# The delta rule's triangular inverses as 64x64 blocks on the array's quarters, in a two-block transformer kernel

## The chip, the core and the metric

The kernel runs as one program on one core of a Trainium2 chip. The core has five engines that run their own instruction streams in order and meet through semaphores: TensorE (PE; its weight loads are listed as PEld), VectorE (DVE), ScalarE (ACT), GpSimd (POOL) and SyncE (SP, which issues the DMAs here). The metric is the device time of one execution in microseconds (us), lower is better.

## The reference, cut to what matters

The program is two transformer blocks on 256 tokens of width 1024. The first (attention and a product-key expert layer) is not touched. In the second, half of the heads are a gated delta rule, computed in chunks of 64 tokens; the other half are a causal sliding window. This is the delta rule, and the window's scores:

```python
# q, k, v: (B, 8 heads, N = 4 chunks, 64 tokens, 64); beta, g: (B, 8, 4, 64)
G = jnp.cumsum(g, axis=-1)
decay = jnp.exp(jnp.where(causal, G[..., :, None] - G[..., None, :], -jnp.inf))
kb = k * beta[..., None]
A = jnp.where(strict, jnp.einsum('bhncd,bhnsd->bhncs', kb, k) * decay, 0.0)
L = A + jnp.eye(64)
rhs = jnp.concatenate([v * beta[..., None], kb * jnp.exp(G)[..., None]], axis=-1)
u, w = split(lax.linalg.triangular_solve(L, rhs, left_side=True, lower=True, unit_diagonal=True))
qk = jnp.where(causal, jnp.einsum('bhncd,bhnsd->bhncs', q, k) * decay, 0.0)
# then, chunk after chunk (state S of 64 x 64 per head):
v_new = u_c - w_c @ S;  o = q_dec_c @ S + qk_c @ v_new;  S = S * dec_c + k_dec_c.T @ v_new
...
# window: 8 query heads, 2 key heads, blocks of 128 queries over their own and the block of keys before
s = einsum(q, k) / 8 - slope_h * dist;  p = exp(s - m) / (sum + exp(sink - m));  o = p @ v
```

There are 8 heads x 4 chunks = 32 unit lower-triangular matrices of 64x64 to invert.

## The kernel before, in words

The tokens lie in two blocks `b` of 128, so a block holds two chunks of 64. Everything is float32; the large products are split in two parts `hi` and `lo` of a rounded type, at L95 and L96, and take three products each (L115 to L117 and L123 to L125). A float32 product of the small kind stands as one instruction in the program and as two matmul records in the trace, each with its weight load; a transpose stands as one and one.

The stretch at issue lies between the projections of the second block and its output projection:

- `conv` (L1006) and what follows it make k, v and q of the delta rule. ScalarE runs SiLU there, and the exponentials are held back behind `zsilu` by `issue_after`.
- L1091 to L1110 make the decay matrices: `Dm` (rows by columns of a block of 128, both chunks in one 128x128 matrix with zero corners) and its transpose `DT`, by products with `ones`, exponentials (L1104) and transposes (L1109).
- `inverse(b, hf, pool)` inverts the eight matrices of block `b` and of four heads (those with the parity `hf`) in 128x128 matrices, two chunks on the diagonal of each. It is a generator that other work is woven into. It starts with k times k transposed (L1147), A (L1153), A's transpose (L1157) and q times k (L1160). Then come five levels, n = 2, 4, 8, 16, 32: a product with A's transpose (L1181) and a mask on VectorE (L1183), a product with the transposed inverse so far (L1188) and a subtraction from T (L1189); T is turned on TensorE (L1174) and copied by ScalarE (L1175). It ends with u and w (L1197, L1198), copied at L1199 and L1200.
- Two such generators, hf = 0 and 1, run in turn (`together`), first for b = 0, then for b = 1.
- `aside` is the window attention in steps: `heads` (L1257) and `window` (L1289: scores L1301 and L1304, maximum L1307, exponentials L1316, division on GpSimd L1321, transposes L1327, product with v L1331). The first ASTEPS of its steps are woven into the inverses of b = 0, the rest into those of b = 1.
- `recur(b)` (L1210) runs the two chunks of a block: L1222 and L1231 with the state, L1237 and L1246 with v_new. `recur(0)` is woven into the inverses of b = 1, `recur(1)` into the window half of the output projection.

A scheduler orders each engine's instructions by what the program order and the pools allow; engines then follow that order. PSUM tiles come from rings: `ps_acc` 4, `ps_mm` 2, `ps_tr` 2. The reciprocal square roots are powers on GpSimd (L142).

Of the kernel before, what the change touches and what calls it, by code (L numbers as in the profile page):

```python
# [10 lines left out]
F32 = mybir.dt.float32  # L11
# [12 lines left out]
D = 1024  # L24
# [5 lines left out]
def tile_kernel(ctx: ExitStack, tc: tile.TileContext, a, out):  # L30
# [792 lines left out]
    for c in range(NCH):  # L823
# [23 lines left out]
        if c == 32:  # L847
# [27 lines left out]
            low = tri("low", BF, 0.0, NEG, True, False)  # L875
# [4 lines left out]
            def half(name, n, first=False):  # L880
                t = cst.tile([128, 64], F32, name=name)
                nc.gpsimd.memset(t, 1.0)
                v = t.rearrange("p (q i) -> p q i", i=n)
                lo, hi = (0, n - 1) if first else (n, 2 * n - 1)
                nc.gpsimd.affine_select(v, v, pattern=[[-2 * n, 64 // n], [0, n]], compare_op=OP.is_ge, fill=0.0,
                                        base=-lo, channel_multiplier=1)
                nc.gpsimd.affine_select(v, v, pattern=[[2 * n, 64 // n], [0, n]], compare_op=OP.is_ge, fill=0.0,
                                        base=hi, channel_multiplier=-1)
                return t

            pair_t = half("pair_t", 1, True)
            halves = {n: half("half%d" % n, n) for n in (1, 2, 4, 8, 16, 32)}
# [71 lines left out]
    with tc.tile_pool(name="b2", bufs=1) as b2:  # L964
# [126 lines left out]
        Dm = b2.tile([128, 2, 8, 128], F32, name="Dm")  # L1091
        DT = b2.tile([128, 2, 8, 128], F32, name="DT")
        for b in range(2):
            gt = b2.tile([128, 4, S], F32, tag="sc", name="gt", bufs=2).rearrange("p h k -> p (h k)").rearrange("p (h t) -> p h t", h=8)
            nc.gpsimd.tensor_tensor(gt, up[:, None, :].to_broadcast([128, 8, 128]),
                                    ngd[:, b, :, None].to_broadcast([128, 8, 128]), op=OP.mult)
            for hf in range(2):
                ps = ps_tr([128, 4, 128])
                nc.tensor.matmul(ps, ones, gt[:, hf * 4:hf * 4 + 4], start=True, stop=False)
                nc.tensor.matmul(ps, identb, low[:, None, :].to_broadcast([128, 4, 128]), start=False, stop=True)  # L1100
                for i in range(4):
                    h = hf * 4 + i
                    with tc.issue_after(zsilu.ins):
                        nc.scalar.activation(Dm[:, b, h], ps[:, i], AF.Exp, bias=Gc[:, b, h:h + 1])  # L1104
        for b in range(2):
            for hf in range(2):
                ps = ps_tr([128, 4, 128])
                for i in range(4):
# [428 lines left out]
```

## Time and profile before

| | |
|---|---|
| three runs | 1450.46, 1441.31, 1449.96 us; median 1449.96 |
| the profiled execution | 1448.03 us, span 1446.3 us |
| busy share of the span: PE, PEld, DVE, ACT, POOL | 94%, 81%, 76%, 51%, 25% |
| matmul records | 8918 |
| DMA, share of 16 engines' span | 52.8% |
| granted TensorE clock | 0.984 of full speed on average |

The busy share of PE is a union of records that overlap, each with its way through the array, so it says that TensorE always had something in flight, and not that it was at its peak. The shares are averages over stages; the stretch of the delta rule and the window lies at about 1100 to 1210 us of the span.

### The profile page before, as it was taken

The numbers are of one execution on the slowest core, as the hardware profiler recorded it, in microseconds if no ns is written. First come the engines' busy times: TensorE is split into PE (matmuls) and PEld (weight loads), VectorE is DVE, ScalarE is ACT, GpSimd is POOL, SyncE is SP. The second block draws the span as 40 slices with busy tenths as digits, with TensorE's granted clock in tenths as the row PEclk, the third lists the DMA queues.
The fourth block names the chain that finished last, engine by engine and source line by source line (L and its number), as shares of the span: only waits on it lengthen the run. The fifth ranks groups of instructions, "written<-read, shape, count | busy, mean of one in ns | idle before, by whom it ended". The sixth has DMA issues, their size and how long they took to land.

```text
span 1446.3 us, 24961 instructions
## 1 busy us (share of the span) xinstructions
PE 1355.2 (94%) x8918; PEld 1178.5 (81%) x8918; DVE 1104.1 (76%) x2345; ACT 741.7 (51%) x1577; POOL 361.1 (25%) x295
## 2 busy tenths in 40 slices
PE   6778799999899999999999999999989999899998
PEld 5535589999899999998777778777787887799997
DVE  7988786889889999978777777788687475755555
ACT  4436455555455544456555555455566233555553
POOL 2224333575633333334101010111143210000000
PEclk9999899999999999999999999999999999999999
DMA  9822255545454545458787788787243002355552
GB/s 360 298 93 99 99 164 169 180 160 175 154 167 162 161 150 172 147 175 304 245 269 262 253 277 274 261 303 258 79 129 119 16 1 88 123 189 184 190 184 79
DMA packets 79389, 259.33 MB, mean 179 GB/s; under 512 B 11680, under 2 KB 15776, under 8 KB 79264
## 3 DMA queue, kind: packets, MB, share of 16 engines
q1 hardware_dynamic: 79264, 257.74, 52.8%
q8 instruction: 70, 1.15, 0.3%
q14 instruction: 55, 0.45, 0.1%
HBM read 256.65 MB, written 1.05 MB: 178 GB/s over the span
## 4 chain that ended last, share of the span: by engine, by line
PE 61%; DVE 17%; DMA 10%; issue 6%; ACT 3%; POOL 3%; DVEq 0%; POOLq 0%; ACTq 0%; SPq 0%
PE ps_mm L123 11%; PE ps_mm L125 10%; PE ps_mm L124 10%; DMA raw<-in_w_ada_dram 6%; PE ps_acc L117 5%; PE ps_acc L115 5%; PE ps_acc L116 5%; DVE lo L96 4%; DVE raw L185 4%; PE ps_tr L730 2%; DMA raw<-in_expert_v_dram 2%; PE ps_acc L1188 1%; PE ps_acc L1181 1%; ACT hi L95 1%; DVE xl L846 1%
## 5 line engine op out<-in xcount | busy, mean ns | idle before, releaser
L95 ACT ACTIVATE hi<-raw 128x512 fp32r<-128x512 f32 (+3 forms) x772 | 473.3, 623 | 398.4 <-PE ps_mm L124 187.4
L96 DVE TENSOR_TENSOR lo<-raw,hi 128x512 fp32r<-128x512 f32 (+2 forms) x614 | 450.6, 745 | 151.5 <-ACT hi L95 147.1
L125 PE MATMUL ps_mm<-hh,lo 128*128 128x256 f32 x1600 | 450.6, 282 | 8.9 <-POOL lo L96 5.9
L123 PE MATMUL ps_mm<-hh,hi 128*128 128x256 f32 x1600 | 454.6, 284 | 2.2 <-DVE hh L235 1.9
L124 PE MATMUL ps_mm<-hl,hi 128*128 128x256 f32 x1600 | 450.5, 282 | 0.0
L96 POOL TENSOR_TENSOR lo<-raw,hi 128x512 fp32r<-128x512 f32 (+1 forms) x158 | 228.7, 1449 | 609.2 <-ACT hi L95 561.6
L125 PEld LDWEIGHTS ps_mm<-hh,lo 128*128 128x128 f32 x1600 | 302.7, 189 | 12.2 <-POOL lo L96 7.4
L123 PEld LDWEIGHTS ps_mm<-hh,hi 128*128 128x128 f32 x1600 | 303.1, 190 | 4.1 <-DVE hh L235 2.5
L124 PEld LDWEIGHTS ps_mm<-hl,hi 128*128 128x128 f32 x1600 | 302.9, 189 | 1.1
L117 PE MATMUL ps_acc<-hi,xl 128*128 128x512 f32 x512 | 203.0, 396 | 8.1 <-DVE xl L846 8.1
L116 PE MATMUL ps_acc<-lo,xh 128*128 128x512 f32 x512 | 202.1, 395 | 2.7 <-DVE lo L96 1.6
L115 PE MATMUL ps_acc<-hi,xh 128*128 128x512 f32 x512 | 201.5, 393 | 0.0
L185 DVE SCALAR_TENSOR_TENSOR raw<-raw,cact 128x1024 f32<-128x1024 f32 x86 | 114.2, 1331 | 49.9 <-DMA raw<-in_w_ada_dram 49.5
L117 PEld LDWEIGHTS ps_acc<-hi,xl 128*128 128x128 f32 x512 | 96.1, 188 | 35.5 <-DVE xl L846 14.5
L116 PEld LDWEIGHTS ps_acc<-lo,xh 128*128 128x128 f32 x512 | 96.2, 188 | 28.0 <-DVE lo L96 3.8
L115 PEld LDWEIGHTS ps_acc<-hi,xh 128*128 128x128 f32 x512 | 96.2, 188 | 21.4
L846 DVE TENSOR_TENSOR xl<-W,xh 128x256 fp32r<-128x256 f32 x128 | 65.1, 511 | 8.0 <-ACT xh L845 7.9
L845 ACT ACTIVATE xh<-W 128x256 fp32r<-128x256 f32 x128 | 52.0, 410 | 37.4 <-PE ps_acc L116 34.8
L117 PE MATMUL ps_acc<-hi,sl 128*128 128x512 f32 x120 | 47.7, 399 | 0.5 <-DVE sl L1371 0.5
L115 PE MATMUL ps_acc<-hi,sh 128*128 128x512 f32 x120 | 47.8, 400 | 0.0
L116 PE MATMUL ps_acc<-lo,sh 128*128 128x512 f32 x120 | 47.5, 396 | 0.0
L739 ACT ACTIVATE W<-ps_tr 128x64 f32<-128x64 f32 (+26 forms) x78 | 20.7, 291 | 47.2 <-DVE W L735 37.5
(402 smaller groups left out, 1787.2 us busy)
## 6 DMA issues: line engine op xcount, KB each, us to landing
raw<-in_expert_u_dram SPq DMA_DIRECT2D x128, 512.0 KB, 3.8
raw<-in_expert_v_dram SPq DMA_DIRECT2D x128, 512.0 KB, 4.5
raw<-in_w_ada_dram SPq DMA_DIRECT2D x96, 512.0 KB, 4.7
raw<-in_w_gate_dram SPq DMA_DIRECT2D x22, 512.0 KB, 3.3
raw<-in_w_up_dram SPq DMA_DIRECT2D x22, 512.0 KB, 3.2
raw<-in_w_down_dram SPq DMA_DIRECT2D x22, 512.0 KB, 3.2
raw<-in_w_out_dram SPq DMA_DIRECT2D x16, 512.0 KB, 3.5
raw<-in_w_query_dram SPq DMA_DIRECT2D x16, 512.0 KB, 3.7
```

The source lines that it names most:

```text
L95: nc.scalar.activation(hi[:, :n], raw[:, c0:c1], AF.Copy)
L96: sub = eng.tensor_sub(lo[:, :n], raw[:, c0:c1], hi[:, :n].bitcast(F32))
L115: nc.tensor.matmul(ps, xh, wh, start=start, stop=False)
L116: nc.tensor.matmul(ps, xh, wl, start=False, stop=False)
L117: nc.tensor.matmul(ps, xl, wh, start=False, stop=stop)
L123: nc.tensor.matmul(ps, wh, hh[:, k], start=k == 0, stop=False)
L124: nc.tensor.matmul(ps, wh, hl[:, k], start=False, stop=False)
L125: nc.tensor.matmul(ps, wl, hh[:, k], start=False, stop=k == KT - 1)
L185: nc.vector.scalar_tensor_tensor(w, w, 1.0, act, op0=OP.mult, op1=OP.mult, accum_out=acc)
L730: nc.tensor.matmul(ps[:, i], o2[:, q + i], o[:, q + i], start=n == 0, stop=n == 1)
L845: nc.scalar.activation(xh, W[:, c], AF.Copy)
L846: nc.vector.tensor_sub(xl, W[:, c], xh.bitcast(F32))
```

## The change

The inverses no longer stand in 128x128 matrices. A block's two chunks lie on the two halves of the partitions, all eight heads in columns of 64, and every product of the inverse is one 64x64 block of one head and one chunk, 16 of them (`tiles4`) to a product of all. The rows of the array that a product uses are set by the partition half of its inputs, the columns by the partition half of its output; the order of `tiles4` takes another quarter with every product. Outputs of the two row halves go to two PSUM tiles. `inverse(b, pool)` treats all eight heads, so there is one generator per block and no longer two. T is turned as a whole at each level; the last turn is a product with the identity, block by block. The decay matrix is made transposed and folded at once, with beta as a second one (`bDT`); A and its transposes are gone. The window's two key heads run in pairs, with scores and products alternating over halves of the array, and ASTEPS is 16 instead of 19.

```diff
+            def folded(name, t, n=64, dt=F32):
+                f = cst.tile([128, n], dt, name=name)
+                nc.gpsimd.tensor_tensor(f, t[:, :n], t[:, n:], op=OP.add)
+                return f
...
-                        nc.scalar.activation(Dm[:, b, h], ps[:, i], AF.Exp, bias=Gc[:, b, h:h + 1])
-        for b in range(2):
-            for hf in range(2):
-                ps = ps_tr([128, 4, 128])
-                for i in range(4):
-                    nc.tensor.transpose(ps[:, i], Dm[:, b, hf * 4 + i], ident)
-                nc.scalar.activation(DT[:, b, hf * 4:hf * 4 + 4], ps, AF.Copy)
+        nc.vector.tensor_scalar(nG, Gc, -1.0, None, op0=OP.mult)
+        sb = small.tile([128, 2, 8], F32, tag="sb", name="sb", bufs=1)
+        with tc.issue_after(zsilu.ins):
+            nc.scalar.activation(sb, gd, AF.Exp)
+        nc.vector.tensor_tensor(sb, sb, beta, op=OP.mult)
...
+            nc.gpsimd.tensor_tensor(gt, spread8(up64, 64), ngd[:, b, :, None].to_broadcast([128, 8, 64]), op=OP.mult)
+            nc.gpsimd.tensor_tensor(bt, spread8(id64, 64), beta[:, b, :, None].to_broadcast([128, 8, 64]), op=OP.mult)
+            ps = ps_tr([128, 8, 64])
+            nc.tensor.matmul(ps, chunk1, gt, start=True, stop=False)
+            nc.tensor.matmul(ps, identb, spread8(past, 64), start=False, stop=True)
+            for h in range(8):
+                with tc.issue_after(zsilu.ins):
+                    nc.scalar.activation(DT[:, b, h], ps[:, h], AF.Exp, bias=nG[:, b, h:h + 1], scale=-1.0)
+            ps = ps_tr([128, 8, 64])
+            nc.tensor.matmul(ps, chunk1, bt, start=True, stop=True)
+            nc.vector.tensor_tensor(bDT[:, b], ps, DT[:, b], op=OP.mult)
...
+        TWO = range(2)
+        P64 = [slice(i * 64, i * 64 + 64) for i in TWO]
+        tiles4 = [(p, i, c) for p in range(4) for i in TWO for c in TWO]
...
-        def inverse(b, hf, pool):
...
+        def inverse(b, pool):
+            ck = [slice(b * 128 + c * 64, b * 128 + c * 64 + 64) for c in TWO]
+
+            def of_keys(other):
+                ps = [ps_acc() for _ in TWO]
+                for p, c, i in tiles4:
+                    nc.tensor.matmul(ps[i][P64[c], p * 64:(p + 1) * 64], kF[P64[i], p, ck[c]], other[P64[i], p, ck[c]],
+                                     start=True, stop=True)
+                return [t[:, :256].rearrange("p (h t) -> p h t", h=4) for t in ps]
+
+            kk = of_keys(kF)
...
+            for i in TWO:
+                nc.vector.tensor_tensor(M[:, i::2], kk[i][:, :, ::2], first1[:, b, i::2], op=OP.mult)
+            nc.vector.tensor_tensor(T[:, :, ::2], T[:, :, ::2], M, op=OP.subtract)
+            for i in TWO:
+                nc.vector.tensor_tensor(AT[:, i::2], kk[i], bDT[:, b, i::2], op=OP.mult)
             yield
...
             for n in (2, 4, 8, 16, 32):
...
+                pt = ps_acc()
+                for p in range(4):
+                    nc.tensor.transpose(pt[:, p * 128:(p + 1) * 128], T[:, 2 * p:2 * p + 2].rearrange("p h t -> p (h t)"), ident)
+                TT = mat("TT", pool).rearrange("p h t -> p (h t)")
+                nc.scalar.activation(TT, pt, AF.Copy)
+                ps = [ps_acc() for _ in TWO]
+                M = b2.tile([128, 4, 2, 32], F32, tag="part", name="part", bufs=2)
+                for p, i, c in tiles4:
+                    nc.tensor.matmul(ps[c][P64[i], p * 32:(p + 1) * 32], AT[P64[c], 2 * p + i], cols(T, n)[P64[c], 2 * p + i],
+                                     start=True, stop=True)
+                for c in TWO:
+                    nc.vector.tensor_tensor(M[:, :, c], ps[c][:, :128].rearrange("p (h t) -> p h t", h=4),
+                                            halves[n][:, None].to_broadcast([128, 4, 32]), op=OP.mult)
                 yield
...
+                for p, c, i in tiles4:
+                    nc.tensor.matmul(ps[i][P64[c], 128 + p * 32:160 + p * 32],
+                                     TT[P64[i], p * 128 + c * 64:p * 128 + c * 64 + 64], M[P64[i], p, c], start=True, stop=True)
+                for i in TWO:
+                    t = cols(T, n)[:, i::2]
+                    nc.vector.tensor_tensor(t, t, compact(ps[i][:, 128:256], n), op=OP.subtract)
                 yield
...
+            for h in range(8):
+                for c in TWO:
+                    nc.tensor.matmul(pt[c][P64[c], h * 64:h * 64 + 64], T[P64[c], h], id64[P64[c]], start=True, stop=True)
+            nc.scalar.activation(TT[P64[0]].rearrange("p h t -> p (h t)"), pt[0][P64[0]], AF.Copy)
+            nc.vector.tensor_copy(TT[P64[1]].rearrange("p h t -> p (h t)"), pt[1][P64[1]])
             yield
...
+            for p, i, c in tiles4:
+                nc.tensor.matmul(pw[c][P64[i], p * 64:(p + 1) * 64], kbe[P64[c], b, 2 * p + i], TT[P64[c], 2 * p + i],
+                                 start=True, stop=True)
+            for c in TWO:
+                nc.scalar.activation(wT[:, :, ck[c]], pw[c][:, :256].rearrange("p (h t) -> p h t", h=4), AF.Copy)
+            pu = [ps_acc() for _ in TWO]
+            for h in range(8):
+                for c in TWO:
+                    nc.tensor.matmul(pu[c][P64[c], h * 64:h * 64 + 64], TT[P64[c], h], vb[P64[c], b, h], start=True, stop=True)
+            for c in TWO:
+                nc.vector.tensor_copy(u[P64[c], b], pu[c][P64[c]])
             yield
...
+                for jj in range(2):
+                    ps = [ps_mm([128, 2, S]) for _ in TWO]
+                    for i in range(2):
+                        for g in TWO:
+                            nc.tensor.matmul(ps[g][:, i, :nk], qT[P64[g], 2 * jj + i, t], kT[P64[g], :nk],
+                                             start=True, stop=True)
...
-        first = inverse(0, 0, b2), inverse(0, 1, b2)
+        first = inverse(0, b2)
...
-        together(inverse(1, 0, dr), inverse(1, 1, dr), r0, aside)
+        together(inverse(1, dr), r0, aside)
...
-ASTEPS = 19
+ASTEPS = 16
```

What the scheduler makes of it, at three places. First TensorE in two levels of the inverses of b = 1. Before (L1181 and L1188 are the products, four of one hf and four of the other, L1174 the turns, L1301 the window's scores, L1327 its transposes):

```order
L1181 MATMUL ps_acc<-T,AT 128x64 x4
L1174 MATMUL ps_acc<-ident,T 128x128 x4
L1181 MATMUL ps_acc<-T,AT 128x64 x4
L1174 MATMUL ps_acc<-ident,T 128x128 x4
L1188 MATMUL ps_acc<-part,TT 128x64 x8
L1181 MATMUL ps_acc<-T,AT 128x64 x4
L1174 MATMUL ps_acc<-ident,T 128x128 x4
L1181 MATMUL ps_acc<-T,AT 128x64 x4
L1174 MATMUL ps_acc<-ident,T 128x128 x4
L1188 MATMUL ps_acc<-part,TT 128x64 x8
```

and now (L1186 turns, L1192 and L1199 products, L1356 the window's transposes, L1361 its product with v):

```order
L1186 MATMUL ps_acc<-ident,T 128x128 x4
L1192 MATMUL ps_acc<-T,AT 64x32 x16
L1356 MATMUL ps_tr<-ident,sc 128x128 x4
L1199 MATMUL ps_acc<-part,TT 64x32
L1356 MATMUL ps_tr<-ident,sc 128x128 x2
L1199 MATMUL ps_acc<-part,TT 64x32 x15
L1356 MATMUL ps_tr<-ident,sc 128x128 x2
L1361 MATMUL ps_mm<-PT,kv 64x512
L1186 MATMUL ps_acc<-ident,T 128x128 x4
L1192 MATMUL ps_acc<-T,AT 64x32 x16
```

Where two halves took turns, one group of 16 now follows the other, with the window's work between the two products of a level.

Second VectorE at the start of b = 1, from the window's scores to the recurrence's first v_new (L1304 scores, L1307 and L1309 to L1312 maximum, L1319 and L1320 the sums, L1153 A, L1163 and L1164 the first level, L1223 v_new). Before:

```order
L1153 SCALAR_TENSOR_TENSOR A<-ps_acc,beta,Dm 128x128 x4
L1304 SCALAR_TENSOR_TENSOR sc<-dist,ps_mm 128x256
L1319 TENSOR_TENSOR sums<-sums,es 128x4
L1304 SCALAR_TENSOR_TENSOR sc<-dist,ps_mm 128x256
L1320 RECIPROCAL sums<-sums 128x4
L1153 SCALAR_TENSOR_TENSOR A<-ps_acc,beta,Dm 128x128
L1307 TENSOR_REDUCE mneg<-sc 128x4
L1153 SCALAR_TENSOR_TENSOR A<-ps_acc,beta,Dm 128x128
L1309 TENSOR_TENSOR mneg<-mneg,sinkB 128x4
L1163 TENSOR_TENSOR part<-A,half_9214 128x256
L1311 TENSOR_TENSOR es<-sinkB,mneg 128x4
L1223 TENSOR_TENSOR vn<-u,ps_tr 64x512
```

and now (L1328 scores, L1333 maximum, L1172, L1173 and L1175 the start of the inverse, L1247 v_new, L1256 the next product with the state):

```order
L1328 SCALAR_TENSOR_TENSOR sc<-dist,ps_mm 128x256 x8
L1333 TENSOR_REDUCE mneg<-sc 128x4
L1172 TENSOR_TENSOR part<-ps_acc,first_12967 128x4x32 x2
L1175 TENSOR_TENSOR AT<-ps_acc,bDT 128x4x64
L1173 TENSOR_TENSOR T<-T,part 128x256
L1175 TENSOR_TENSOR AT<-ps_acc,bDT 128x4x64
L1247 TENSOR_TENSOR vn<-u,ps_tr 64x512
L1333 TENSOR_REDUCE mneg<-sc 128x4
L1256 TENSOR_TENSOR u<-ps_tr,eq 64x512
```

The rows now are without a break: all eight scores of the window's second block and one maximum stand ahead of the inverse's start. Before, the four scores of one key head were woven into the making of A, and the other four came later.

Third ScalarE in the convolutions: now an exponential for `sb` (L1104) stands among the SiLUs (L1022).

```order
L95 ACTIVATE hi<-raw 128x512
L1104 ACT_TABLE_LOAD
L1104 ACTIVATE sb<-gd 128x16
L1017 ACTIVATE cx<-ps_mm 128x256
L1019 ACTIVATE cy<-ps_mm,convw 128x256
L1022 ACT_TABLE_LOAD
L1022 ACTIVATE F<-cy 128x256
```

Before, the first exponential came behind the last SiLU; two table loads are new here.

## Rows read from the trace of the kernel before

**Rows 1.** Busy time by stretch: stretch, length, busy (instructions) per engine, PE clock, DMA

```profile
1103.00:1121.00 18.00, 17.98 (x92) 12.38 (x91) 13.68 (x31) 12.41 (x32) 10.20 (x10) 1.00 0.26 89
1121.00:1155.00 34.00, 33.49 (x263) 29.79 (x262) 16.38 (x50) 9.95 (x27) 8.01 (x8) 1.00 0.05 17
1155.00:1210.00 55.00, 53.49 (x414) 43.80 (x413) 33.52 (x90) 19.18 (x55) 8.14 (x6) 1.00 0.00 1
```

**Rows 2.** Chain of waits, one level for b = 1: start, length, engine, line

```profile
1185.66 0.89 PE ps_acc L1181 x8
...
1188.28 1.73 PE ps_acc L1188 x16
1190.02 0.89 PE ps_acc L1181 x8
```

**Rows 3.** Chain of waits, marks of the two inverses' stretches

```profile
1121.89 0.17 PE ps_acc L1181 x2
...
1154.91 0.36 PE ps_acc L1198 x2
...
1179.91 1.03 PE ps_acc L1181 x8
...
1203.71 0.26 PE ps_acc L1197 x2
...
1210.36 1.02 PE ps_tr L1222 x8
```

**Rows 4.** Chain of waits, hand-overs between TensorE and VectorE in a level

```profile
1145.01 0.43 DVE T L1189
...
1145.49 0.66 PE ps_acc L1174 x4
```

**Rows 5.** Chain of waits, recurrence of b = 0, second chunk

```profile
1175.69 1.08 PE ps_tr L1237 x8
1176.78 1.07 PE ps_tr L1246 x16
```

**Rows 6.** Timeline of PE: start, length, line, form (rows*columns of the array)

```profile
1165.46 0.27 PE L1237 MATMUL ps_tr<-vn,kd 64*128 64x128 f32 x1
1165.46 0.27 PE L1160 MATMUL ps_acc<-F,kF 64*128 64x128 f32 x1
...
1163.78 0.59 PE L1331 MATMUL ps_mm<-PT,kv 128*64 128x512 f32 x1
1163.79 0.38 PE L1231 MATMUL ps_tr<-Sb,F 128*64 128x128 f32 x2
```

**Rows 7.** Groups by form, 1040 to 1250: count, busy, mean ns, idle before

```profile
L1189 DVE TENSOR_TENSOR T<-T,ps_acc 128x256 f32<-128x256 f32 x20 | 8.4, 421 | 8.9 <-PE ps_acc L1188 8.8
L1304 DVE SCALAR_TENSOR_TENSOR sc<-dist,ps_mm 128x256 f32<-128x256 f32 x8 | 3.1, 418 | 0.5 <-PE ps_mm L1301 0.5
L1223 DVE TENSOR_TENSOR vn<-u,ps_tr 64x512 f32<-64x512 f32 x4 | 2.7, 684 | 2.3 <-PE ps_tr L1222 2.3
L1307 DVE TENSOR_REDUCE mneg<-sc 128x4 f32<-128x1024 f32 x2 | 2.4, 1211 | 0.0
L1304 DVE SCALAR_TENSOR_TENSOR sc<-dist,ps_mm 128x128 f32<-128x128 f32 x8 | 1.9, 283 | 3.8 <-PE ps_mm L1301 3.8
L142 POOL TENSOR_TENSOR rstd<-ms,mhalf 128x10 f32<-128x10 f32 x2 | 4.3, 2138 | 4.1 <-DVE ms L141 4.1
L1016 ACT ACT_TABLE_LOAD x1 | 1.3, 1283 | 0.0
```

**Rows 8.** Chain of waits, decay matrices and start of b = 0

```profile
1110.19 1.08 PE ps_acc L1147 x8
1111.27 1.02 PE ps_tr L1109 x8
...
1117.55 1.08 PE ps_acc L1160 x8
```

**Rows 9.** Timeline of ACT in the convolutions, with idle time before

```profile
1078.39 0.42 ACT L1016 ACTIVATE F<-cy 128x256 f32<-128x256 f32 x1 [0.92 <-DVE cy L1015]
```

More of the change, by code (lines that the diff above doesn't have):

```diff
@@ L1105, in tile_kernel @@
-        for b in range(2):
-            for hf in range(2):
-                ps = ps_tr([128, 4, 128])
-                for i in range(4):
-                    nc.tensor.transpose(ps[:, i], Dm[:, b, hf * 4 + i], ident)
-                nc.scalar.activation(DT[:, b, hf * 4:hf * 4 + 4], ps, AF.Copy)
+        DT = b2.tile([128, 2, 8, 64], F32, name="DT")
+        bDT = b2.tile([128, 2, 8, 64], F32, name="bDT")
+        first1 = b2.tile([128, 2, 8, 32], F32, name="first1")
+        nG = small.tile([128, 2, 8], F32, tag="nG", name="nG", bufs=1)
@@ L1292, in window @@
                 nk = 128 * (b + 1)
-                po = ps_mm()
-                for g in range(2):
-                    hp = slice(g * 64, g * 64 + 64)
-                    sc = b2.tile([128, 4, S], F32, tag="sc", name="sc", bufs=2)
-                    mneg = small.tile([128, 4], F32, tag="mneg", name="mneg", bufs=2)
-                    for jj in range(2):
-                        ps = ps_mm([128, 2, S])
-                        for i in range(2):
-                            nc.tensor.matmul(ps[:, i, :nk], qT[hp, 2 * jj + i, t], kT[hp, :nk], start=True, stop=True)
+                sc = [b2.tile([128, 4, S], F32, tag="sc", name="sc", bufs=2) for _ in TWO]
@@ L1314, in window @@
-                    sums = small.tile([128, 4], F32, tag="sums", name="sums", bufs=2)
+                            nc.vector.scalar_tensor_tensor(sc[g][:, 2 * jj + i, :nk], dist[:, 256 - nk:],
+                                                           -(2.0 ** -(h + 1)), ps[g][:, i, :nk], op0=OP.mult, op1=OP.add)
+                    yield
+                mneg, es, sums = (small.tile([128, 8], F32, tag=n, name=n, bufs=2) for n in ("mneg", "es", "sums"))
+                for g in TWO:
+                    nc.vector.tensor_reduce(mneg[:, g * 4:g * 4 + 4], sc[g][:, :, :nk], axis=AX.X, op=OP.max)
@@ L1330, in window @@
                         yield
[L1331 removed]
+                    for g in TWO:
+                        nc.tensor.matmul(po[P64[g]], kv[:, kb, 128 + g * 64:192 + g * 64], PT[g], start=kb == 0, stop=kb == b)
                 nc.scalar.activation(oT[:, :, t], po.rearrange("p (j t) -> p j t", j=4), AF.Copy)
@@ L1339, in tile_kernel @@
             if k in (3, 6):
-                for g in first:
-                    next(g)
+                next(first)
         share["pool"] = 0.0
@@ L1346, in tile_kernel @@
         dr = tc.alloc_tile_pool(name="dr", bufs=1, side="right")
-        together(*first, (next(aside, None) for _ in range(ASTEPS)))
+        together(first, (next(aside, None) for _ in range(ASTEPS)))
         r0 = recur(0)
-        together(inverse(1, 0, dr), inverse(1, 1, dr), r0, aside)
+        together(inverse(1, dr), r0, aside)
         dr.release()
@@ L1441 @@
 GT = 8
-PARTS = 4
 ASHARE = 0.34
```

150 lines of the change are left out of this document (52 added, 98 removed).

## The prediction, written before the changed kernel was run

> **What bounds the kernel now.** I read the page's slices first: TensorE is busy in nearly all of them, so only a stretch in which its own work shrinks, or in which it waits in small steps, can move the time. Then the table by stretch [rows 1]: in the decay matrices and the start of b = 0 TensorE is busy for 17.98 of 18.00 us, in the inverses of b = 0 for 33.49 of 34.00 and in those of b = 1 for 53.49 of 55.00, with VectorE at 33.52 there; the clock is at its upper level, 2.4 GHz, throughout (1.00). So the kernel is bound by TensorE's instructions here, and not by their waits: two halves take turns and cover each other's masks. Then the chain of waits, for one level [rows 2]: from 1185.66 to 1190.02 us, 4.36 us, in which only TensorE rows stand. Then its marks [rows 3]: the inverse's work for b = 0 runs from 1121.89 to the end of L1198 at 1155.27 (33.4 us); from there to the first L1181 of b = 1 at 1179.91 it is 24.6; from there to L1197 at 1203.71 it is 23.8; and 6.65 more to L1222 of the last recurrence at 1210.36. Last the timeline, for what two blocks of the array do at once [rows 6].
>
> The profiled execution took 1448.03 us, 1.9 below the median of the three runs (1449.96, between 1441.31 and 1450.46). The sum goes against 1448.03.
>
> **The price of a small product.** Sixteen records of L1246 (eight products of 64x64 over 64 columns, one block of the array) take 1.07 us, and eight records with a 128-wide block take 1.08 [rows 5]: 67 ns for a record of the first kind, 135 for the second. L1237 and L1160 use different row halves and start in one instant, 1165.46, with the same 0.27 us each; L1331 and L1231, on different column halves, start 0.01 us apart [rows 6]. So two blocks work at once. Four at once, in turn with every product, stand in no row. A group of 16 products is 32 records: 2.14 us if one follows the other, 1.07 with pairs at once, 0.54 with all four. 32 columns in place of 64 I cost like 64, since a record's weights stay as many. I take 1.07, for pairs are what the rows show, and keep 0.54 and 2.14 as bounds.
>
> **A level.** Transposes 0.66 [rows 4], product 1.07, two masks of half the size (0.28 each by the 128x128 form, L1304) [rows 7], product 1.07 and 0.2 until its last result is out (a record lasts 0.27 [rows 6] and the next starts 0.07 later), two subtractions 0.57, and four hand-overs of 0.03 to 0.05 (L1189 ends at 1145.44, TensorE starts at 1145.49 [rows 4]): 0.66 + 1.07 + 0.57 + 1.27 + 0.57 + 0.16 = **4.30 us**, against 4.36 now. One generator per block means that TensorE has nothing of the inverse to do under masks and subtractions, some 1.3 us a level; the window's and recurrence's work fills part. So the gain in products is given back level by level as waiting. The change must gain elsewhere.
>
> **Part by part.**
> (a) Decay matrices and start of b = 0, TensorE full. Gone: 16 transposes L1109 at 1.02 per eight [rows 8], 2.0 us; eight of L1157, 1.0. L1147 and L1160, 8 products each for all heads, are 32 records at 1.08 per eight [rows 8], 4.3 us, and become two groups, 2.1. That is 5.2; the modes that now alternate with 128-wide work cost a little. I take −5, bounds −3 and −6. VectorE (13.68 of 18) and ScalarE (12.41) cover their new and lost passes [rows 1].
> (b) Inverses of b = 0, 33.4 now. After: five levels 21.5. The end: turn by a group 1.27, copy 0.68 (64x512 form of L1223 [rows 7]) and two hand-overs 0.1, then pw and pu 2.14: 4.2. In VectorE's stream the two heads' reciprocal square roots, powers of 2.14 us on GpSimd (L142) [rows 7], stand ahead of the subtractions of the first two levels; half of each lies under the product, so 2.3 more with its hand-overs. The window's own steps (scores, exponentials ahead of the copy of TT, GpSimd's division ahead of the transposes, the product with v) lie partly in the path: no row gives it for the new order; between 0 and GpSimd's whole 8.01 us of this stretch [rows 1] I take 4.0, the middle. Sum 32.0, so −1.4 (bounds −5.4 and +2.6).
> (c) From there to the first level of b = 1, 24.6 now: two generators, the recurrence's first chunks and the window's scores run through VectorE one behind the other. After, in the order shown: eight scores 3.1 (0.42 each), two maxima 2.4, the start (two of 0.28, three of 0.42) 1.8, v_new, its next product and o 3 x 0.68 = 2.05, four passes of 0.42 for the state and q times k 1.7 [rows 7]: 11.1. Then a first mask and the products that it lets through: 0.57 + 0.05 + 1.27, and L1237 and L1246, 2.15 [rows 5]: 4.0. Sum 15.1, so **−9.5**. A's passes are gone. The cover for all this is that nothing new waits ahead of them; without it, see the second rival.
> (d) Levels of b = 1, 23.8 now. After: four more levels 17.2, the turn 2.05, one power on GpSimd 2.0, the window's transposes and product with v 2.5 (estimates, bounded as in (b)): 23.75, so 0.
> (e) End of b = 1, 6.65 now: pw 1.27, hand-over 0.03, two copies at 0.4 each: 2.1, so −4.5; u is needed later.
> (f) ScalarE loads its table of functions twice more, since `sb` stands among SiLUs: 1.28 us a load [rows 7], 2.6. ScalarE idles between 0.9 us waits on VectorE there [rows 9], so part is hidden: +2.0, bounds 0 and 2.6.
> SyncE's DMA order stays; GpSimd loses the copies and updates of TT, which are not in the path. What comes behind, output projection and feed-forward, stays. Sum: −5 − 1.4 − 9.5 − 0 − 4.5 + 2.0 = −18.4, so 1429.6: **1430**, by its own bounds 1422 to 1439. Chance 0.42.
>
> **Rivals.**
> First: all four quarters at once. A group takes 0.54; 27 groups lie in the path, 20 in the levels and seven others (two in (a), three in (b), one each in (d) and (e)), so 27 x 0.53 = 14.3 less, of which the powers' waits of (b) and (d), 2.3 and 2.0, take 4.3 back, since the products that cover them are shorter: −10 on the forecast, **1420**. For it: row pairs and column pairs both run freely [rows 6]. Against: no more than two records stand together in these rows. Chance 0.25. The Trainium skill, "TensorEngine Tiling (Array Packing)", Theoretical Speedup and Tiling Configurations, lists four independent 64x64 tiles; no row of before shows four.
> Second: the change does not bring what it says, because the in-order streams keep (c) as long as it is: VectorE's eight scores and a maximum (4.6 us) now stand ahead of the inverse [rows 7], and the window's and recurrence's chains wait for one another. Then (c) gives 0 and the rest −8.9: **1439**. For it: 33.5 of 55 us of VectorE are busy in this stretch [rows 1]. Against: A's passes, 16 of them, go. Chance 0.16.
> Third, the other side: quarters do not overlap. A group costs 2.14, so the 27 groups add 28.9, of which the 4.3 of the powers' waits are covered: +24.6, **1454**, slower than before. It decides from a group of about 1.9 us (119 ns a product): there (18.4 + 4.3) / 27 = 0.84 are added to 1.07. For it: alternating modes at L1198 take 0.36 us for two records [rows 3], more than 0.27. Against: the pairs [rows 6]. Chance 0.15. The Trainium skill, "TensorEngine Tiling (Array Packing)", Instruction Overhead, speaks against the change: it states some 60 cycles for each product however few its columns, and that no tiling factor should be taken from a dimension that is already small, which 64 columns cut to 32 are. By that rule a group saves nothing for its 32 columns, and the sum is 1430, as I have it; were the cost in proportion to the columns, a group would take 0.54 and the sum would be the first rival's 1420. No row of before has 32 columns with 64x64 blocks.
> Fourth: each change of quarter empties the array as L1198 shows, 0.36 us for a product of two records [rows 3], 5.8 us a group: 27 x 4.7 = +127, **1556**. Against: a mode is the blocks' size, and that stays. Chance 0.02.
>
> **How the numbers follow.** 1% of the median is 14.5 us, about what a measurement of this kernel can tell from no change; faster by that is below 1435.5, slower above 1464.5. Faster: of the forecast 0.7 (its range crosses 1435.5), of the first rival 0.95, of the second 0.1: 0.29 + 0.24 + 0.02, with a little for gains not listed, 0.57. Slower: the fourth 0.02, of the third 0.25, and 0.03 for waits in the streams beyond the second: 0.09. The same: 0.34. The range, 1414 to 1451, takes in the forecast, the first rival with 6 us below, the second, and the cheaper part of the third; left out is what lies above and a little below.
>
> **What would show it.** In the profile after: a group of 16 rows of L1192 or L1199 in the chain of 1.07 us (1.0 to 1.2) shows pairs, 0.5 to 0.7 four at once, over 1.9 the third rival. A level, from one L1186 to the next, of 4.3 us where no window work is woven in. TensorE's busy share over the levels falls below 0.9, with idle time ended by VectorE. From the end of pw of b = 0 to the first L1192 of b = 1 15 us; over 22 shows the second rival. The decay stretch shorter by 5 us. Two table loads among the convolutions, with SiLUs later by about 1 us each. What would make the sum wrong: a level longer than 5 us through ScalarE's exponentials ahead of the copy of TT, or the output projection starting later than the recurrence because its weights' transfers are not there.

## The result, and the profile after

The changed kernel takes 1424.36 us (median of 4 runs, 1421.52 to 1426.86) against 1450.20 of the kernel before: a ratio of 0.9835, 95% interval 0.9810 to 0.9861. Forecast were 1430 and a range of 1414 to 1451. The profiled execution took 1425.19 us, its span 1423.4.

The time comes from other places than the sum had it. The table takes TensorE's marks in the two profiles (us); a stretch ends where the next begins, and the last transpose of the convolutions is L1027 before and L1033 now. The prediction calls 1179.91 us the first L1181 of b = 1; the timeline has that one at 1167.40, and at 1179.84 the second level begins, from which the table counts.

| stretch | before | changed | measured | forecast |
|---|---|---|---|---|
| start to the last transpose of the convolutions | 1099.08 | 1090.74 | −8.3 | +2.0 (f) |
| to the first level of b = 0: decay matrices | 22.65 | 24.62 | +2.0 | −5 (a) |
| to the end of the last L1197, now L1222, of b = 0 | 33.19 | 30.72 | −2.5 | −1.4 (b) |
| to the second level of b = 1 | 24.92 | 18.74 | −6.2 | −9.5 (c) |
| to the last block's recurrence | 30.45 | 23.87 | −6.6 | −4.5 (d, e) |
| to the last product | 230.54 | 229.60 | −0.9 | 0 |

Before, one L1198 of 0.36 us still follows the last L1197 of b = 0; counted to its end, the third row is −2.8 and the fourth −5.8.

First the size of a group. This is the chain of waits of the changed kernel, at two levels of b = 0 and b = 1 (start, length, engine, tile, line); the rows answer to [rows 2, 4]:

```profile
1125.44 1.04 PE ps_acc L1186 x4
1126.48 1.01 PE ps_acc L1192 x32
...
1172.10 0.60 PE ps_acc L1192 x32
...
1174.72 0.60 PE ps_acc L1199 x32
...
1176.33 0.59 PE ps_acc L1186 x4
```

The same 32 records take 1.01 us in one place and 0.60 in the other, and four transposes 1.04 and 0.59. The table by stretch of the changed kernel says why; its columns are those of [rows 1], and the last number but two is the granted clock:

```profile
1101.00:1104.00 3.00, 0.38 (x2) 0.00 (x0) 2.96 (x5) 1.96 (x9) 3.00 (x3) 0.97 0.00 0
1104.00:1107.00 3.00, 1.86 (x3) 0.86 (x4) 2.99 (x8) 0.00 (x0) 1.37 (x2) 0.50 0.00 0
1107.00:1110.00 3.00, 3.00 (x9) 2.32 (x8) 0.69 (x1) 0.63 (x1) 0.00 (x0) 0.50 0.55 175
1119.00:1122.00 3.00, 1.86 (x38) 1.63 (x39) 2.56 (x10) 0.60 (x1) 0.51 (x1) 0.81 0.04 14
1122.00:1125.00 3.00, 2.72 (x40) 2.29 (x39) 1.76 (x9) 0.69 (x1) 1.45 (x1) 0.50 0.02 5
1128.00:1131.00 3.00, 3.00 (x40) 2.32 (x40) 0.53 (x3) 0.69 (x1) 0.00 (x0) 0.50 0.00 0
1140.00:1143.00 3.00, 2.61 (x60) 2.36 (x53) 0.77 (x4) 1.05 (x6) 1.33 (x2) 0.50 0.02 5
1146.00:1149.00 3.00, 3.00 (x15) 1.36 (x12) 1.38 (x2) 1.19 (x2) 0.00 (x0) 1.00 0.00 0
```

Before, the clock stood at 2.4 GHz (1.00) in all of this [rows 1]. Now TensorE works for 0.38 of 3 us from 1101, and then the clock is at 1.2 GHz (0.50) until about 1110; it falls again about 1121 and stays there until 1145, also where TensorE's rows fill a stretch to 3.00 of 3.00. It falls twice more in b = 1, each time for about 3 us (1169 to 1172 and 1186 to 1189). Ahead of both long stretches at 1.2 GHz TensorE stood idle. TensorE's timeline names the two waits (in brackets idle time before, and what ended it):

```profile
1105.14 2.04 PE L1122 MATMUL ps_tr<-gt,chunk 128*128 128x512 f32 x2 [3.75 <-DVE bDT L1123]
...
1116.72 0.77 PE L1199 MATMUL ps_acc<-part,TT 64*64 64x32 f32 x32 [0.70 <-DVE part L1195]
1120.14 0.66 PE L1186 MATMUL ps_acc<-ident,T 128*128 128x128 f32 x4 [2.65 <-DVE T L1203]
```

The second is VectorE's queue, as (b) had it: a reader of the power (L1292) stands ahead of the subtraction. VectorE's timeline:

```profile
1118.99 0.17 DVE L1292 TENSOR_SCALAR rstd<-rstd 128x8 f32<-128x8 f32 x1 [2.13 <-POOL rstd L142]
1119.07 0.28 DVE L1299 TENSOR_TENSOR q<-kv,rstd 128x128 f32<-128x128 f32 x1
1119.27 0.42 DVE L1296 TENSOR_TENSOR q<-ps_mm,rstd 128x256 f32<-128x256 f32 x1
1119.61 0.48 DVE L1203 TENSOR_TENSOR T<-T,ps_acc 128x128 f32<-128x128 f32 x2
```

The first is new. L1122 of b = 1 needs the ps_tr tile that VectorE's L1123 of b = 0 reads, and that stands behind passes which are slow there. VectorE and, under it, GpSimd at the same time:

```profile
1101.02 2.45 DVE L1250 TENSOR_TENSOR Sd<-Sb,dec 64x256 f32<-64x256 f32 x2
1103.50 0.89 DVE L1236 TENSOR_TENSOR eq<-eG,rq 128x8 f32<-128x8 f32 x1
```

```profile
1100.96 2.23 POOL L1130 TENSOR_TENSOR kbe<-kn,be 128x512 f32<-128x512 f32 x2
1103.15 1.22 POOL L1114 TENSOR_TENSOR gt<-id,beta 128x512 f32<-128x512 f32 x1
```

A pass of L1250 takes 1.22 us while GpSimd works, and 0.43 where it does not, as in the chain later:

```profile
1161.43 0.43 DVE Sd L1250
```

Behind L1122 in TensorE's stream waits the projection (L115 to L117), so all of TensorE waits.

### The profile page after: what moved, and what is told of

It reads as the page before. It is cut to its first block, busy times and chain, and to the rows that moved or that the text cites. A ratio compares the mean times of both kernels' runs of the same rounds, so it can differ in the third digit from the quotient of the medians.

```text
span 1423.4 us, 25768 instructions
## 1 busy us (share of the span) xinstructions
PE 1326.3 (93%) x9356; PEld 1153.3 (81%) x9356; DVE 1090.6 (77%) x2323; ACT 737.0 (52%) x1562; POOL 354.1 (25%) x291
## 4 chain that ended last, share of the span: by engine, by line
PE 63%; DVE 15%; DMA 9%; issue 6%; POOL 4%; ACT 2%; DVEq 0%; POOLq 0%; ACTq 0%; SPq 0%
PE ps_mm L123 11%; PE ps_mm L125 11%; PE ps_mm L124 11%; DMA raw<-in_w_ada_dram 7%; PE ps_acc L117 6%; PE ps_acc L115 6%; PE ps_acc L116 6%; DVE lo L96 4%; DVE raw L185 3%; PE ps_tr L730 2%; DMA raw<-in_expert_v_dram 1%; POOL W L662 1%; POOL lo L96 1%; POOL rstd L142 1%; ACT hi L95 1%
## 5 line engine op out<-in xcount | busy, mean ns | idle before, releaser
L117 PE MATMUL ps_acc<-hi,xl 128*128 128x512 f32 x512 | 202.1, 395 | 10.0 <-DVE xl L846 9.8
L116 PE MATMUL ps_acc<-lo,xh 128*128 128x512 f32 x512 | 201.2, 393 | 1.0 <-POOL lo L96 0.6
L115 PE MATMUL ps_acc<-hi,xh 128*128 128x512 f32 x512 | 200.6, 392 | 0.0
L117 PEld LDWEIGHTS ps_acc<-hi,xl 128*128 128x128 f32 x512 | 96.5, 188 | 36.1 <-DVE xl L846 16.1
L116 PEld LDWEIGHTS ps_acc<-lo,xh 128*128 128x128 f32 x512 | 96.4, 188 | 24.6 <-DVE lo L96 2.0
L115 PEld LDWEIGHTS ps_acc<-hi,xh 128*128 128x128 f32 x512 | 96.6, 189 | 19.9
L115 PE MATMUL ps_acc<-hi,sh 128*128 128x512 f32 x120 | 47.8, 400 | 0.3 <-ACT sh L1399 0.3
L117 PE MATMUL ps_acc<-hi,sl 128*128 128x512 f32 x120 | 47.3, 395 | 0.1
L116 PE MATMUL ps_acc<-lo,sh 128*128 128x512 f32 x120 | 47.2, 393 | 0.0
```

The lines of the kernel that those rows point to most:

```text
L115: nc.tensor.matmul(ps, xh, wh, start=start, stop=False)
L116: nc.tensor.matmul(ps, xh, wl, start=False, stop=False)
L117: nc.tensor.matmul(ps, xl, wh, start=False, stop=stop)
```

## Experiments

The theory after reading: the four quarters do work at once, so a group takes 0.60 us at 2.4 GHz (the first rival's price); what that should have brought went into waits that TensorE no longer covers, and into the clock that falls after them. Beside the time, each kernel is measured by its profile from the last transpose of the convolutions to the last product, since what lies ahead scatters from execution to execution: 341.8 us before, 327.5 in the changed kernel. This is one execution of each kernel. gp_load (below), which changes nothing in this stretch but GpSimd's work at its start, has 325.8, so a difference under 2 us in it says nothing.

**The order of the quarters (serial).**

```diff
-        tiles4 = [(p, i, c) for p in range(4) for i in TWO for c in TWO]
+        tiles4 = [(p, i, c) for i in TWO for c in TWO for p in range(4)]
```

> The 16 products of a group come quarter by quarter, four of one quarter in a row, in place of another quarter with every product. Theory: the alternation lets the four blocks work at once (0.60 us for 32 records of L1192 in the changed kernel, 19 ns a record). In a row of one quarter a record takes the 67 ns of L1246: a group 2.1 us, 27 groups in the path 1.5 us longer each, +40 us, less 5 to 15 us since TensorE then idles less and keeps its upper clock: 1449 to 1465 us. Rival: the rate comes from the small products (32 columns) and not from their order: a group stays at 0.6 and the time at 1424, within 5 us.

1443.89 us, ratio to before 0.9976 (0.9952 to 0.9999); 344.3 us in the stretch. TensorE's chain at 2.4 GHz in that kernel, with the level that answers to the rows above:

```profile
1191.77 1.40 PE ps_acc L1199 x32
```

and its table by stretch in the inverses of b = 0:

```profile
1128.00:1132.00 4.00, 4.00 (x40) 3.61 (x39) 1.91 (x8) 0.69 (x1) 0.00 (x0) 0.50 0.02 4
1140.00:1144.00 4.00, 4.00 (x42) 3.38 (x40) 0.78 (x3) 0.60 (x1) 0.00 (x0) 0.50 0.01 4
1164.00:1168.00 4.00, 4.00 (x23) 3.00 (x23) 2.29 (x7) 0.60 (x1) 0.00 (x0) 1.00 0.02 4
```

A group takes 1.40 us instead of 0.60. So the alternation makes the rate, and nearly all of the change's gain: without it 1444 remain. The size was off, 1444 for the 1449 to 1465 expected, and the starts of the single records say why. On one quarter they start 58 ns apart, with the 32 columns of this L1199 as with the 64 of L1246 in the kernel before; the 67 ns of the prediction had the group's start in them. Where serial goes from one quarter to the next, the last records of the one overlap with the first of the other, so 32 records take 1.40 us and not 2.1. In the changed kernel four records, one of each quarter, start 3 to 7 ns apart, and the next four 58 ns later at most places. And the clock stays at 0.50 in stretches that TensorE's rows fill wholly; it is back at 1.00 from about 1161.6 us, under the window's transposes (L1356, from 1160.79).

**The wait at L1122 (one_buffer, then bt_acc).**

```diff
-            gt, bt = (b2.tile([128, 4, S], F32, tag="sc", ...)[:, :512] ... for _ in range(2))
+            g2 = b2.tile([128, 4, S], F32, tag="sc", name="gt", bufs=2).rearrange("p h k -> p (h k)")
+            gt, bt = (g2[:, i * 512:i * 512 + 512].rearrange("p (h t) -> p h t", h=8) for i in range(2))
```

> Both inputs of the decay products of a block (gt and bt) lie in the two halves of one buffer, so GpSimd need not wait for a buffer before it makes those of b = 1. Theory: the 3.75 us that TensorE idles ahead of L1122 in the changed kernel go, with them the half clock from 1103 to 1111 us (0.50 in the rows) under the projection: 5 to 8 us less than the changed kernel, 1417 to 1420. Rival: the projection behind it waits for its operands anyway (ScalarE's hi, or the transfers), and the wait only moves: within 2 us of 1424.

1423.35 us (0.9848, 0.9816 to 0.9880), 325.9 in the stretch: 1.7 less, not 5 to 8. I had put the wait on GpSimd's buffer, though the row names VectorE's L1123, and in this kernel it is still there:

```profile
1102.80 2.08 PE L1122 MATMUL ps_tr<-gt,chunk 128*128 128x512 f32 x2 [3.32 <-DVE bDT L1123]
```

bt_acc takes away what the row names, too:

```diff
-            ps = ps_tr([128, 8, 64])
+            ps = ps_acc([128, 8, 64])
             nc.tensor.matmul(ps, chunk1, bt, start=True, stop=True)
```

> As one_buffer, and the product L1122 writes into a tile of the ring ps_acc and no longer of ps_tr. In one_buffer TensorE still waited at L1122 of b = 1, for VectorE's L1123 that frees the ps_tr tile and that stands behind four slow passes; the buffer of GpSimd was not what ended the wait. Theory: that wait (3.75 us in the changed kernel) and the half clock from 1104 to 1111 us go: 5 to 7 us less than the changed kernel, 1417 to 1419. Rival: VectorE's and GpSimd's passes (kbe, kd, L1250) in this place end last anyway, since the first level needs bDT: 0 to 2 us, 1422 to 1425.

1425.03 us (0.9847, 0.9815 to 0.9879), 324.1 in the stretch. The decay stretch is 19.83 us, 4.8 less than in the changed kernel and 2.8 less than before, so (a) had the right sign where this wait is gone. A wait of 1.92 us for VectorE is left in the place, with the clock at 0.50 behind it, and 1.4 us come back in the inverses of b = 0.

```profile
1105.34 0.67 PE L116 MATMUL ps_mm<-lo,hh 128*128 128x512 f32 x1 [1.92 <-DVE lo L96]
```

What is left of the gain cannot be seen in the medians.

**The wait at the powers (heads_first, heads_held).**

```diff
+                with tc.issue_after(behind["T"]):
                     nc.vector.tensor_scalar(r[:, :8], r[:, :8], 0.125, None, op0=OP.mult)
```

Here `behind["T"]` is the last subtraction (L1203) of the level at hand; the two sums of squares come first.

> The two powers of the heads' reciprocal square roots are issued one behind the other, and VectorE's instruction that reads the first stands behind the subtraction of the level at hand and no longer ahead of it. Theory: the 2.65 us that TensorE idles ahead of the second L1186 in the changed kernel go, and since it then has work without a break the granted clock stays at 1.00 and does not fall to 0.50 from 1121 to 1145 us: 2.6 + 5 to 8 us less, 1414 to 1417. Rival: the clock falls anyway, since a level leaves TensorE idle under every mask: 2 to 3 us less, 1421 to 1422, with 0.50 still in the rows.

1425.11 us, 327.9 in the stretch: a miss, since another reader of the same power went ahead and waited there (TensorE's idle time 2.62 us as before). heads_held puts all readers behind:

> As heads_first, but all of VectorE's readers of the powers (L1298, L1301 and L1304), and not the first alone, stand behind the subtraction of the level at hand; in heads_first L1305 went ahead of it and waited there, with TensorE idle for 2.62 us as before. Theory: that wait is gone, 2.0 to 2.6 us; with it the fall of the clock at 1122 us comes later or not at all, 0 to 8 us more: 1415 to 1423, most likely 1420. Rival: VectorE's wait stands ahead of the next mask (L1196) in its place, and nothing is gained: 1423 to 1426.

1424.98 us (0.9828, 0.9794 to 0.9862), 327.1. In its timeline the wait of 2.65 us has become two:

```profile
1122.88 0.65 PE L1187 MATMUL ps_acc<-ident,T 128*128 128x128 f32 x4 [0.58 <-DVE T L1204]
1123.47 0.67 PE L1193 MATMUL ps_acc<-T,AT 64*64 64x32 f32 x32
1125.26 0.82 PE L1309 MATMUL ps_tr<-ident,q 128*128 128x128 f32 x4 [1.12 <-DVE q L1301]
```

and then the clock falls. Shorter waits alone did not hold it up here.

**Work in the waits (fill, combo3).** fill adds products that nobody reads:

```diff
+        def fill(n):
+            ps = ps_acc([128, 8, 64])
+            for _ in range(n):
+                nc.tensor.matmul(ps, identb, spread8(past, 64), start=True, stop=True)
...
                 r = rstd_of(ssq, 10, 64)
+                fill(12)
```

> The changed kernel with 24 products more that nobody reads (128x128 by 512 columns in a two-byte type), twelve behind the sum of squares of each of the heads' two blocks, where TensorE waits for the powers on GpSimd (they come ahead of L1199 of the first two levels, 0.22 us each, 5.3 us in all, of which 3.4 and 1.3 us fall into waits that are there already). Theory: the granted clock fell to 0.50 at 1121 because TensorE stood idle; with work in the waits it stays at 1.00 from 1121 to 1145 us, where some 17 us of TensorE's rows are in the chain: 6 to 8 us saved, 1 to 2 us paid, 1418 to 1420 us. Rival: it falls anyway, since the products of a level use a quarter of the array for short: 0.50 in the rows as before, and 1 to 3 us more, 1425 to 1428.

1430.20 us (0.9884, 0.9859 to 0.9909), 327.9 in the stretch: no gain in the stretch, and a median 6 us above the changed kernel's (the profile took its fastest execution, 1425.30, so it does not show where these 6 us lie). The rows show both sides. The first twelve ended before the wait did (3.39 us idle ahead of the second level), and the clock fell; of the second twelve the first four started about 427 ns apart, at 0.50, and the others 216 ns, at 1.00, where the clock then stayed for some 13 us:

```profile
1120.00:1123.00 3.00, 0.47 (x5) 0.23 (x3) 0.83 (x5) 0.69 (x1) 1.96 (x1) 1.00 0.00 0
1123.00:1126.00 3.00, 2.14 (x37) 1.75 (x38) 1.40 (x6) 0.60 (x1) 0.00 (x0) 0.63 0.02 5
1126.00:1129.00 3.00, 3.00 (x12) 1.14 (x12) 0.49 (x2) 0.00 (x0) 0.00 (x0) 0.81 0.00 0
1129.00:1132.00 3.00, 3.00 (x77) 2.29 (x75) 0.84 (x3) 1.07 (x2) 0.00 (x0) 1.00 0.00 0
```

From the third L1186 of b = 0 to L1209, three levels, it took 10.4 us (1130.92 to 1141.35), the changed kernel at 0.50 15.7 (1125.37 to 1141.04), of which 1.3 are five transposes (L1304, L1307) that stand ahead of the third level in fill. combo1 and combo2 first put the shorter waits together: both are bt_acc with heads_held; combo1 has this as well (`decx` is the exponential of dec),

```diff
-        with tc.issue_after(zsilu.ins):
+        with tc.issue_after(decx.ins):
             nc.scalar.activation(sb, gd, AF.Exp)
```

and combo2 this in its place (`behind["M"]` is the level's last mask):

```diff
+                with tc.issue_after(behind["M" if b == 0 else "T"]):
                     nc.vector.tensor_reduce(ssq, q2, axis=AX.X, op=OP.add)
```

> bt_acc and heads_held together, and the exponential for sb behind the other exponentials, so that no table is loaded among the SiLUs. Theory: the three do not overlap in place: -5 to -7, -2 to -3 and, since VectorE and not ScalarE sets the convolutions' pace, 0 to -1 for the two loads: 1414 to 1418 us. Rival: one wait hides the other (the projection ends earlier only to wait longer at the powers): 1420 to 1423.

> bt_acc and heads_held, and the sum of squares of the heads' first block stands on VectorE behind the first mask and no longer ahead of it (in bt_acc TensorE stood idle for 1.86 us ahead of the first L1199, since that sum waits for ScalarE's squares). No change to the exponential for sb. Measured from the last transpose of the convolutions to the last product, the changed kernel takes 327.5 us, bt_acc 324.1, combo1 322.5. Theory: -1.5 against combo1, so 321, if the clock falls in the levels of b = 0 as before; 316 if it stays up, since TensorE then has no wait over 0.8 us there. Rival: the waits only move: 322 to 324.

combo1: 1421.56 us (0.9827, 0.9796 to 0.9859), 322.5 in the stretch. combo2: 1422.20 (0.9821, 0.9790 to 0.9851), 324.2; the clock falls as before (0.50 from about 1116 to 1146), and the rival is right. combo3 is combo2 with three products of `fill` behind each group of 16, in four levels of b = 0 and two of b = 1:

> combo2 with 36 products that nobody reads (128x128 by 512 columns), three behind each group of 16 in four levels of b = 0 and the last two of b = 1, where TensorE waits for masks and subtractions (0.6 to 0.8 us a time; three products are 0.66 us). Theory: the clock stays at 1.00 in both inverses; in the kernel fill three levels of b = 0 took 10.4 us at 1.00 where the changed kernel took 15.7 at 0.50, so 5 us here, 1 to 2 more in b = 1, less 1 to 2 where the added products delay the next group: 314 to 317 us from the last transpose of the convolutions to the end. Rival: the added products cost what the clock brings: 320 to 323.

1417.76 us, 0.9787 (0.9756 to 0.9818), and 316.4 in the stretch: 7.8 less than combo2 and 11.1 less than the changed kernel, by work that computes nothing. Its clock, and one level of its timeline:

```profile
1117.00:1120.00 3.00, 2.73 (x44) 1.68 (x42) 2.34 (x7) 1.58 (x4) 0.61 (x1) 1.00 0.94 362
1120.00:1123.00 3.00, 1.95 (x39) 1.19 (x39) 2.64 (x7) 1.23 (x4) 0.82 (x1) 1.00 0.18 57
1126.00:1129.00 3.00, 3.00 (x77) 2.56 (x72) 2.13 (x9) 1.18 (x2) 0.72 (x1) 1.00 0.02 5
```

```profile
1131.10 0.66 PE L1192 MATMUL ps_acc<-ident,T 128*128 128x128 f32 x4
1131.68 0.67 PE L1198 MATMUL ps_acc<-T,AT 64*64 64x32 f32 x32
1132.29 0.82 PE L1161 MATMUL ps_acc<-past,identb 128*128 128x512 bf16 x3
...
1135.11 0.66 PE L1192 MATMUL ps_acc<-ident,T 128*128 128x128 f32 x4
```

The row of combo2 at the same mark:

```profile
1120.00:1123.00 3.00, 2.80 (x40) 2.77 (x41) 1.67 (x9) 0.54 (x1) 1.64 (x1) 0.50 0.02 5
```

The inverses of b = 0 take 24.3 us instead of combo2's 30.2, at 1.00 throughout, with idle time still there (1.95 of 3 us busy). The added products are the only difference between the two, so the half clock costs 6 us net in this stretch, shown by its removal. It is not the profiled execution alone: the mean granted clock is 0.973 to 0.980 in the five executions of combo3 behind its interval and 0.963 to 0.975 in the six of combo2. combo3 is the fastest version; its median lies 6.6 us below the changed kernel's, and the two intervals overlap.

What makes the clock fall is not settled. combo3 waits at L116 as bt_acc does, and its clock stays at 1.00 there, as in combo2:

```profile
1112.30 0.50 PE L116 MATMUL ps_mm<-lo,hh 128*128 128x512 f32 x1 [1.92 <-DVE lo L96]
```

**The window alone, and 16 steps (window_alone, steps16).** The kernel before with the changed `window` and ASTEPS = 16, and with the last alone:

```diff
-ASTEPS = 19
+ASTEPS = 16
```

> The kernel before with the window's new order alone (key heads in pairs, 16 steps in the first inverses). Theory: the gain is the inverses'; the pairs alone give 0 to 3 us, 1447 to 1450. Rival: the pairs give the gain, by scores that overlap on two row halves (16 groups of scores at half the time, 4 to 6 us) and by fewer small passes on VectorE and ScalarE: 1440 or less. A second question: the changed kernel reached the end of the convolutions 8.3 us earlier (last L1027, 1098.80 to 1090.46 us), ahead of all that it changes on TensorE. If that is the scatter of executions, this kernel, equal to the one before up to there, and the other three, equal to the changed one, scatter over 1090 to 1099 alike; if the change brings it, this one stands at 1097 to 1100 and the others at 1089 to 1092.

> The kernel before with 16 steps of the window in the first inverses in place of 19, the number of the changed kernel. Theory: no effect of its own, within 2 us of the kernel before. It also tells, by a third profile that equals the kernel before up to 1100 us, whether the stretch of the experts' second matrices, 865 to 971 us, is always longer there (105.6 and 110.2 us so far, 101.5 to 104.5 in eight profiles of changed ones), as something in the program would make it: 105 to 110; or by chance: 101 to 110.

window_alone: 1454.13 us, 1.0056 (1.0035 to 1.0077). steps16: 1452.03, 1.0029 (1.0005 to 1.0053). Both are slower by a little, so neither the window's order nor the 16 steps gives the gain by itself; in the stretch they take 340.6 and 343.8 us. On the second question: the convolutions end at 1101.7 and 1094.9 us in these two, and at 1090.2 to 1099.4 in the eleven profiles of kernels with the change, so this mark scatters. But inside it one stretch does not overlap: the experts' second matrices, by the starts of the same two transfers, take 105.6, 110.2 and 108.5 us in the three kernels that equal the one before up to there, and 101.5 to 104.5 in the eleven others. VectorE, ScalarE and GpSimd have the same number of instructions there. What makes it so is open; it is some 5 us of the 26 (by the means of the two sets).

**GpSimd in the convolutions (gp_load).**

```diff
+            idle = b2.tile([128, 4, S], F32, tag="sc", name="idle", bufs=2)...
+            nc.gpsimd.tensor_tensor(idle, up[:, None, :].to_broadcast([128, 8, 128]), ngd[:, b, :, None].to_broadcast([128, 8, 128]), op=OP.mult)
```

> The changed kernel with two multiplications more on GpSimd, 128x1024 each, of the kind and at the place of those that the kernel before had there (gt of 128 columns); nobody reads them. Theory: the convolutions became shorter with the change because GpSimd's passes slow VectorE's while both run (L1015 586 ns on average before, L1021 548 now): from the transfer that opens the convolutions to their last transpose 77.4 us before and 74.7 in the changed kernel; here 76.5 to 78, with the time 1426 to 1428. Rival: it is something else (the order of ScalarE's loads, memory places): 74 to 75 as in the changed kernel.

1424.42 us (0.9860, 0.9814 to 0.9906). The convolutions took 75.7 us, between the 74.7 of the changed kernel and the 77.4 of the one before. Only one of the two passes fell into them (the other ran at 1100.60). VectorE's pass of the convolution (mean ns of one behind the busy time) was slower by some of the difference:

```profile
L1021 DVE SCALAR_TENSOR_TENSOR cy<-cx,convw,cy 128x256 f32<-128x256 f32 x36 | 20.2, 564 | 1.3 <-ACT cy L1019 0.8
```

against 548 ns in the changed kernel and 586 before. That fits the theory, but does not show it: bt_acc, combo2 and combo3 have 564 ns too, without the added passes, and 73.9 to 75.3 us. What parts the profiles more clearly is the exponential for `sb`. The ten kernels that have it among the SiLUs, with the two table loads, take 73.3 to 75.7 us; the three that do not have it take 76.7 to 77.3, and combo1, which has all else of the change but moves it behind the SiLUs, takes 76.4, with 580 ns. So the rival (the order of ScalarE's loads) is the likelier one, by a single profile of combo1; how it would act is open.

## Why the prediction was right, and where it was not

The direction and the size came out, 1424 for 1430. The sum behind it did not, and part of the agreement is luck. For (a) to (e), −20.4 were forecast and −13.3 measured, although the groups were cheaper than forecast: a new wait and the half clock took back more than that. Ahead of them the profile was 8.3 us shorter, where +2.0 was forecast; 3.5 us of this (5 by the means of all profiles) lie in the experts' stretch, with no known cause. The forecast's own upper bound, 1439, does not follow from the bounds given for (a), (b) and (f), which end at 1436.

- **The price of a group.** Forecast 1.07 us, pairs at once; measured 0.60 at 2.4 GHz. The first rival had it (0.54). The Trainium skill, "TensorEngine Tiling (Array Packing)", Key Properties, says that tiles work independently of one another; the trace agrees, 1.40 us with four products in a row on one quarter against 0.60. Its section Instruction Overhead, which I set beside the third rival, would have 32 columns cost as much as 64; the trace agrees with that, too: on one quarter records start 58 ns apart with either, and a group in alternation takes 0.62 us with 64 columns (L1163) and 0.60 with 32. So the first rival's price came from the four quarters, and the assumption that 32 columns cost like 64 held.
- **The clock.** No term and no rival had it. I read 1.00 in all rows of before [rows 1] and took it for given, while forecasting that TensorE would stand idle for 1.3 us a level. That is the step that failed in (b): at the first rival's price (b) would have been about −6 (13 groups at 0.53 less, 2.3 of it covered), and the lower clock, which costs 6 us from combo3 to combo2, took most of it back. With the clock up (combo3, which has two shorter waits as well) the stretch of b = 0 is 8.9 us shorter than before, and not 2.5.
- **(a), the decay matrices.** −5 forecast, +2.0 measured. The step that failed is that VectorE and ScalarE cover their new and lost passes. A product in TensorE's stream had come to wait for a VectorE pass behind four long ones, which busy shares (13.68 of 18 us) cannot show. With that wait taken away (bt_acc) the stretch is 2.8 us shorter than before, just short of the bound of −3.
- **(c) −9.5 and (d, e) −4.5**: −6.2 and −6.6, together −12.8 for −14.0. A level without other work in b = 1 takes 2.93 us (1180.94 to 1183.87) and not 4.30; 0.94 of the 1.37 are its two groups at 0.60. The second rival (c as long as before) fell.
- **(f), the table loads.** +2.0 forecast; the two loads are there, and the convolutions are 2.7 us shorter all the same. Taking the loads away (combo1) made them no shorter but about 2 us longer, so the sign of (f) was wrong, by one profile; why is not shown.
- **The third rival** is what serial shows, at a smaller price per record: without the alternation almost nothing is left of the gain, and in that kernel's stretch 2.5 us are lost against the kernel before.

## What to carry to other kernels

When TensorE's work gets shorter, ask at what clock the rest will run: look for the waits that its work used to cover, and price them by what may follow them at half the clock, not by their own length alone. Products on the array's quarters overlapped fully only when every product took another quarter, so write the order down and test it by itself. And read the releaser in the row before choosing an experiment: it named VectorE, and I changed GpSimd's buffer first.

## What the runs showed of the hardware

- Records of 64x64 blocks in alternating quarters take 0.60 / 32 = 19 ns each on average at 2.4 GHz and 32 ns at 1.2. By their starts (L1192 at 1172.03) four records of four quarters follow one another within 3 to 7 ns and the next four about 48 ns behind, so that each quarter starts one every 58 ns; at 1.2 GHz that is 107 ns. The Trainium skill, "TensorE: Matmul & The Clock Gate", section "Wait — 56ns, not 53.3ns?", says that start-to-start never drops below about 25 ns; that does not hold here between records on different quarters, and no two on one quarter come closer than 50 ns in these rows.
- The clock stayed at 1.2 GHz for 24 us in which TensorE's rows were mostly full of small products (3.00 of 3.00 at 1128, 4.00 of 4.00 in serial). It came back at about 1144.8 under 64-column products (L1215) and in serial under transposes, in both ahead of the wide ones. With three wide products that nobody reads behind the groups of four of the five levels it was at 2.4 GHz throughout the inverses of b = 0, with TensorE idle for 3.2 of 24.3 us there, against 3.4 of 41.7 in serial and 5.6 of 30.2 in combo2, both mostly at 1.2 GHz.
- A VectorE pass of 64x256 took 1.22 us beside a GpSimd multiplication and 0.43 without.
